# Token rows for the expert pairs: one-hot products replaced by an indirect DMA, and a weight ring of 20 slots

## The chip, the cores and the metric

One NeuronCore of a Trainium2 chip runs the whole kernel. The metric is device time in microseconds (us), the median of several runs. TensorE (PE) multiplies matrices and loads its stationary operand beside that (PEld); VectorE (DVE), ScalarE (ACT) and GpSimd (POOL) do the elementwise work; SyncE (SP) issues most of the transfers. Sixteen DMA engines move the data of all queues.

## The reference, cut to what matters

One decoder layer: four token mixers on 512 tokens of 1024 channels, merged and projected by `w_out`, then a mixture of experts. Only the last part and its routing are touched:

```python
g_prob = softmax(hf @ wg + bg);  g_p, g_idx = top_k(g_prob, 1)         # 4 groups
top_v, top_i = top_k(logits_of_that_group, 2)                          # 2 of 8 experts
gate = g_p * softmax(top_v);     expert = g_idx * 8 + top_i            # 1024 choices in all
y = (silu(xe @ w1[e]) * (xe @ w3[e])) @ w2[e]                          # per expert, D 1024, hidden 512
out[token] += gate * y
```

`hf` is the normalised residual stream, scaled by `a2` and shifted by `sh2` per channel. There are 32 experts with 6 MB of float32 weights each; all weights are read.

## The kernel before, in words

The mixers and the output projection take the first 815 us. The output projection works on two halves of the tokens (two tiles of 128 each); after each half `route` (line 1137) normalises, picks the experts of that half's tokens, and gives each choice a rank within its expert. The place of a choice is its slot: expert times 64 plus rank. Two experts make a pair, so a pair has 128 slots, and 16 pairs follow one another. Choices with a rank of 64 or more go to `overflow` (line 1403), a loop whose trip count is read from a table at run time.

How a pair gets its tokens: `route` keeps the normalised tokens as two fp16 halves (`xh`, `xl`, lines 1148 to 1162; in half 1 POOL subtracts). For two pairs at a time (a group) `rows` (line 1097) builds one-hot masks `pg` on DVE, and `gather` (line 1105) multiplies the halves with them on TensorE: 64 products of 128x256 per group, which leave the tokens transposed in PSUM. ACT and DVE then apply `a2` and `sh2` (lines 1494 and 1496) into `xe`. `tables` (line 1315) makes, for each pair, the gates `ga` (by small products `pq` and DVE steps) and the transposed mask `pT` (by four transposes `pr` and a copy on ACT).

`front` (line 1337) multiplies `xe` with the pair's w1 and w3 into `ph`, and forms g. `Back` (line 1354) transposes g (`gTp`), multiplies with w2 (`py`), scales and splits the result in two parts (`parts`), and `add` multiplies with `pT` and adds into `xm` on DVE: eight times per pair, with two products `po` each.

The weights come in 198 loads, issued by SP in order (line 1072) into a ring of 18 slots of 1 MB: ten of their own, six of the weight buffers of the stage before, and two of the buffers `ml` of the merged activations (lines 1061 to 1063). A load waits until TensorE has done with what its slot held. The order on TensorE in this stage is the order written out in the loop over pairs (line 1505 on), under a manual schedule; DVE is under one only during `route` of half 1. While `route` of half 1 runs on DVE, `meanwhile` (line 1115) gives TensorE the first half of group 0's gather and a few spare products. Once per program, `a2` and `sh2` are written to DRAM as columns and read back in another order (lines 1024 to 1031, POOL's queue).

Of the kernel before, what the change touches and what calls it, by code (L numbers as in the profile page):

```python
# [9 lines left out]
F32 = mybir.dt.float32  # L10
# [27 lines left out]
def trunk(ctx, tc, x, c, ada_w, ada_b, norm1_g, norm2_g, w_in, hgrn_lb, hgrn_norm_g, conv_w, conv_b, conv_ln_g,  # L38
# [24 lines left out]
    cst = ctx.enter_context(tc.tile_pool(name="cst", bufs=1))  # L63
    ps_mm = ctx.enter_context(tc.tile_pool(name="ps_mm", bufs=3, space=PSUM))
# [835 lines left out]
    a2c = cst.tile([128, KD], F32, name="a2c")  # L900
    sh2c = cst.tile([128, KD], F32, name="sh2c")
# [106 lines left out]
    io = keep.tile([128, 256], F16, name="io")  # L1008
    P.iota(io, pattern=[[1, 256]], base=0, channel_multiplier=0, allow_small_or_imprecise_dtypes=True)
# [52 lines left out]
    ring[RL[0]:RL[0]] = [(late, "ml")]  # L1062
    ring[RL[1]:RL[1]] = [(late, "ml")]
# [33 lines left out]
    def rows(g, p_, ts):  # L1097

        s4 = keep.tile([128, 2, NT], F32, name="s4", bufs=2)
        for t in ts:  # L1100
            V.tensor_scalar(s4[:, :, t], slot[:, 0:2, t], -256.0 * g, None, op0=OP.add)
            V.tensor_scalar(p_[:, t], io, s4[:, 0, t:t + 1], None, op0=OP.is_equal)
            V.scalar_tensor_tensor(p_[:, t], io, s4[:, 1, t:t + 1], p_[:, t], op0=OP.is_equal, op1=OP.add)

    def gather(p_, pv_, ts, ds):

        for d in ds:
            if d // 4 not in pv_:
                pv_[d // 4] = psz("xeps").rearrange("p a (b c) -> p (a b) c", c=256)
            o = pv_[d // 4][:, d % 4]  # L1110
            for t in ts:
                mm(o, xr[t][0][:, d * 128:(d + 1) * 128], p_[:, t], t == 0 and d % 2 == 0, False)
                mm(o, xr[t][1][:, d * 128:(d + 1) * 128], p_[:, t], False, t == NT - 1)

    def meanwhile(p_, pv_):


        scr = psm("scr")

        def spare(n):  # L1120
            for _ in range(n):
                mm(scr, ident, xm[:, 0, :512], True, True)

        spare(WARM[0])
        yield
        spare(WARM[1])
        for ds in ((0, 1, 2, 3), (4, 5), (6, 7)):
            gather(p_, pv_, (0, 1), ds)
            a = yield
            mm(scr[:a.shape[-1], :2], a, ident[:, :2], True, True)  # L1130
        spare(WARM[2])
        yield

    xr = []
    sq2 = nr.tile([128, NT, 4], F32, name="sq2")

    def route(half, pl, between=None):
# [5 lines left out]
        r10 = nr.tile([128, 2], F32, name="r10", bufs=2)  # L1143
        V.reduce_sum(v, sq2[:, ts], axis=AX.X)
        rsqrt(r, v, 1.0 / D)

        V.tensor_scalar(r10, r, 1024.0, None, op0=OP.mult)
        xhl = late.tile([128, 2, 2, D], F16, name="xhl", tag="mh")
        for i in range(2):
            xh, xl = xhl[:, i, 0], xhl[:, i, 1]  # L1150
            by_k = lambda a: a.rearrange("q (a p k) -> q a k p", p=128, k=4)
            in_k = lambda a: a.rearrange("q (a k p) -> q a k p", p=128, k=4)
            xi = by_k(xm[:, 2 * half + i])
            A.activation(in_k(xh), xi, AF.Copy, scale=r10[:, i:i + 1])
            if half:
                xs = nr.tile([128, D], F32, name="xs")
                A.activation(in_k(xs), xi, AF.Copy, scale=r10[:, i:i + 1])
                P.tensor_sub(xl, xs, xh)
            else:
                for a in range(2):  # L1160
                    V.scalar_tensor_tensor(in_k(xl)[:, a], xi[:, a], r10[:, i:i + 1], in_k(xh)[:, a], op0=OP.mult, op1=OP.subtract)
            xr.append((xh, xl))
        lg = nr.tile([128, 2, 36], F32, name="lg", bufs=2)
# [8 lines left out]
        el = nr.tile([128, 2, 8, 4], F32, name="el", bufs=2)  # L1172
# [22 lines left out]
        V.tensor_mul(oo, oo, pp.rearrange("p (o t e) -> p o t e", o=1, e=32).to_broadcast([128, 2, 2, 32]))  # L1195
        V.reduce_sum(rank[:, :, ts], oo, axis=AX.X)
        then(rank[:, 1, ts])
        rk, sl = rank[:, :, ts], slot[:, 0:2, ts]
        q = nr.tile([128, 2, 2], F32, name="q4", bufs=2)
        V.tensor_scalar(q, rk, 64.0, None, op0=OP.is_lt)  # L1200
        V.scalar_tensor_tensor(sl, eid[:, :, ts], 64.0, rk, op0=OP.mult, op1=OP.add)
        V.scalar_tensor_tensor(sl, sl, 1.0, q, op0=OP.add, op1=OP.mult)
        V.tensor_scalar(sl, sl, -1.0, None, op0=OP.add)
        if half:
            rows(0, first[0], (2, 3))
# [10 lines left out]
        gh, gl = (sg[:, 2:6, ts].rearrange("p (k a) t -> p a k t", a=2)[:, a] for a in range(2))
        V.tensor_scalar(gf, slot[:, 2:4, ts], 2.0 ** 15, None, op0=OP.mult)
        V.tensor_copy(gh, gf)
        V.tensor_sub(gf, gf, gh)
        V.tensor_scalar(gl, gf, 2.0 ** 11, None, op0=OP.mult)  # L1220
# [18 lines left out]
    for half in range(2):  # L1239
# [38 lines left out]
    def overflow_tables():  # L1278
# [12 lines left out]
        tmp32 = moe.tile([128, 32], F32, name="tmp32", bufs=1)  # L1291
# [20 lines left out]
    moe = ctx.enter_context(tc.tile_pool(name="moe", bufs=2))  # L1312
    ew = stream()

    def tables(p, p_):

        so = p % 2 * 128
        pr, pq = ps_mm.tile([128, 1024], F16, name="pr", tag="mm"), psm("pq")
        for t in range(NT):
            mm(pq[:, :6], p_[:, t, so:so + 128], sg[:, :, t], t == 0, t == NT - 1)  # L1320
        for t in range(NT):
            T.transpose(pr[:, t * 128:(t + 1) * 128], p_[:, t, so:so + 128], ident16)

        ga = moe.tile([128, 4], F32, name="ga")
        two = pq[:, 2:6].rearrange("p (k a) -> p a k", a=2)
        V.tensor_scalar(ga[:, 0:1], pid, 128.0 * p, None, op0=OP.add)
        V.tensor_scalar(ga[:, 1:2], pq[:, 0:1], ga[:, 0:1], 2.0 ** -15, op0=OP.is_equal, op1=OP.mult)
        V.tensor_copy(ga[:, 2:4], two[:, 0])
        V.scalar_tensor_tensor(ga[:, 2:4], two[:, 1], 2.0 ** -11, ga[:, 2:4], op0=OP.mult, op1=OP.add)
        V.tensor_mul(ga[:, 0:1], ga[:, 1:2], ga[:, 2:3])  # L1330
        V.scalar_tensor_tensor(ga[:, 3:4], ga[:, 1:2], 2.0 ** -15, ga[:, 3:4], op0=OP.subtract, op1=OP.mult)
        V.tensor_sub(ga[:, 0:1], ga[:, 0:1], ga[:, 3:4])
        pT = moe.tile([128, 512], F32R, name="pT")
        A.activation(pT, pr[:, :512], AF.Copy)
        return ga, pT

    def front(p, ga, xe):

# [225 lines left out]
```

## Time and profile before

| | |
|---|---|
| median of 3 runs | 1344.1 us (1340.98 to 1345.77) |
| the profiled execution's own time | 1340.95 us |
| its span, first to last instruction | 1339.1 us |
| mean granted clock of TensorE | 0.978 |
| busy: TensorE, DVE, ACT, POOL | 95%, 54%, 35%, 15% of the span |
| DMA | 292.99 MB, mean 219 GB/s |

A row of the timeline gives the start, the duration of a merged run of like instructions, engine, line, operation, output and input; what stands in brackets is the idle time of the engine just before, and what ended it. Matmuls are pipelined, so the duration of a run is a little longer than the distance to the next run's start. Windows give busy times in a stretch, the granted clock as a share of 2.4 GHz (0.5 is 1.2 GHz), and the mean busy share and rate of the DMA engines.

### The profile page before, as it was taken

To read this page: it belongs to the slowest core of one execution; us is meant where nothing else is said; L and a number is where in the kernel's file an instruction comes from. 1 tells how busy PE (TensorE), PEld (TensorE's weight loads), DVE (VectorE), ACT (ScalarE), POOL (GpSimd) and SP (SyncE) were. 2 spreads that over 40 slices of the span, in tenths; PEclk is the share of its full clock that TensorE was granted. 3 is DMA by queue.
4 is the path that set the end of the run, shared out by engine and by line. 5 is a ranking of instruction groups with operands and counts; after the bars stand their busy time and mean duration, and the time that the engine had idled before them with its cause. 6 is when DMAs were issued, how large, how long until landed. Compare 5 with 4: busy or idle time off the path is not lost. (4 is left out here: it accounts for less than half of the span.)

```text
span 1339.1 us, 18010 instructions
## 1 busy us (share of the span) xinstructions
PE 1270.5 (95%) x7265; PEld 894.4 (67%) x7265; DVE 718.5 (54%) x1264; ACT 471.0 (35%) x651; POOL 200.7 (15%) x157
## 2 busy tenths in 40 slices
PE   7999998999999999999989998899999999999997
PEld 5789887987789887878767896243544445353534
DVE  2624579998955555479544565253343433334324
ACT  4448464454546365454314544010111111011100
POOL 3135746001010112031111201000000000000000
PEclk9999998999999999999989999899999999999998
DMA  9432211122122232257764584999999999999961
GB/s 340 131 99 88 71 64 32 64 66 93 63 84 75 63 95 92 66 187 241 186 201 133 190 333 169 379 369 420 395 420 395 418 410 420 395 409 420 397 213 64
DMA packets 105633, 292.99 MB, mean 219 GB/s; under 512 B 8408, under 2 KB 63800, under 8 KB 81740
## 3 DMA queue, kind: packets, MB, share of 16 engines
q1 hardware_dynamic: 102312, 289.45, 57.6%
q10 hardware_dynamic: 2724, 2.26, 0.5%
q8 instruction: 58, 0.95, 0.3%
q0 software_dynamic: 512, 0.12, 0.1%
q14 instruction: 27, 0.22, 0.0%
HBM read 289.69 MB, written 2.11 MB: 218 GB/s over the span
## 5 line engine op out<-in xcount | busy, mean ns | idle before, releaser
L58 PE MATMUL ph<-ew,xe 128*64 128x512 f32 x1024 | 222.5, 592 | 0.8 <-ACT xe L1496 0.8
L58 PE MATMUL mm<-hh,wl 128*128 128x512 f32 x448 | 176.2, 393 | 4.5 <-DVE wl L253 2.9
L58 PE MATMUL mm<-hh,wh 128*128 128x512 f32 x448 | 180.0, 402 | 0.0
L58 PE MATMUL mm<-hl,wh 128*128 128x512 f32 x448 | 175.6, 392 | 0.0
L253 DVE TENSOR_TENSOR wl<-raw,wh 128x2048 fp32r<-128x2048 f32 x55 | 129.6, 2357 | 80.2 <-ACT wh L252 80.2
L58 PEld LDWEIGHTS ph<-ew,xe 128*64 128x64 f32 x1024 | 73.3, 137 | 146.8 <-issue 145.8
L1398 DVE TENSOR_TENSOR xm<-xm,po 128x512 f32<-128x512 f32 (+1 forms) x136 | 84.9, 650 | 158.2 <-PE po L58 157.1
L252 ACT ACTIVATE wh<-raw 128x2048 fp32r<-128x2048 f32 x55 | 105.1, 1911 | 76.2 <-PE mm L58 76.0
L58 PE MATMUL mm<-wh,hh 128*128 128x256 f32 x448 | 130.0, 290 | 0.0
L58 PE MATMUL mm<-wl,hh 128*128 128x256 f32 x448 | 127.1, 284 | 0.0
L58 PE MATMUL mm<-wh,hl 128*128 128x256 f32 x448 | 127.0, 283 | 0.0
L58 PE MATMUL py<-ew,gT 128*64 128x512 f32 (+1 forms) x544 | 118.8, 591 | 5.8 <-issue 5.1
L58 PEld LDWEIGHTS mm<-hh,wh 128*128 128x128 f32 x448 | 84.9, 190 | 24.0 <-issue 7.6
L58 PEld LDWEIGHTS mm<-hh,wl 128*128 128x128 f32 x448 | 84.6, 189 | 23.3 <-DVE wl L253 3.3
L58 PEld LDWEIGHTS mm<-hl,wh 128*128 128x128 f32 x448 | 84.9, 190 | 16.8 <-DVE hl L205 0.3
L58 PEld LDWEIGHTS mm<-wh,hh 128*128 128x128 f32 x448 | 86.1, 192 | 6.0 <-issue 5.8
L58 PEld LDWEIGHTS py<-ew,gT 128*64 128x64 f32 x544 | 39.1, 143 | 75.5 <-issue 72.5
L58 PEld LDWEIGHTS mm<-wl,hh 128*128 128x128 f32 x448 | 86.2, 192 | 0.2
L58 PEld LDWEIGHTS mm<-wh,hl 128*128 128x128 f32 x448 | 86.1, 192 | 0.0
L156 ACT ACTIVATE yh<-py 128x512 fp32r<-128x512 f32 (+1 forms) x34 | 19.4, 572 | 152.8 <-DVE py L1386 152.8
L1386 DVE TENSOR_TENSOR py<-py,g2b 128x512 f32<-128x512 f32 (+1 forms) x34 | 22.7, 668 | 86.0 <-PE py L58 85.5
L1349 ACT ACTIVATE g<-ph 128x512 f32<-128x512 f32 x16 | 9.6, 598 | 165.2 <-PE ph L58 165.2
(441 smaller groups left out, 2166.9 us busy)
## 6 DMA issues: line engine op xcount, KB each, us to landing
ew<-in_expert_w_dram SPq DMA_DIRECT2D x186, 1024.0 KB, 11.4
raw<-in_w_in_dram SPq DMA_DIRECT2D x26, 1024.0 KB, 5.0
raw<-in_w_gate_dram SPq DMA_DIRECT2D x16, 1024.0 KB, 5.5
adaw<-in_ada_w_dram SPq DMA_DIRECT2D x64, 256.0 KB, 3.4
aw<-in_ada_w_dram SPq DMA_DIRECT2D x32, 256.0 KB, 5.4
raw<-in_w_branch_dram SPq DMA_DIRECT2D x8, 1024.0 KB, 5.5
raw<-in_w_out_dram SPq DMA_DIRECT2D x6, 1024.0 KB, 5.9
ew<-in_expert_w_dram SPq DMA_DIRECT2D x12, 512.0 KB, 5.9
```

Source lines behind the costliest of these rows:

```text
L58: T.matmul(o, l, r, start=start, stop=stop, skip_group_check=True)
L156: A.activation(h_ap, src, AF.Copy)
L252: a = A.activation(wh, raw, AF.Copy)
L253: v = V.tensor_sub(wl, raw, wh.bitcast(F32))
L1349: A.activation(g, ph[:, 0], AF.Sigmoid)
L1386: V.tensor_mul(py, py, g2b[:, cs])
L1398: V.tensor_add(xm[:, t, cs], xm[:, t, cs], po)
```

## The change

In `route` ACT now writes the normalised tokens in float32 into one SBUF tile (`xg0`, two passes per half), and each tile of 128 tokens is written to a DRAM buffer `xhd`. Small products with one-hot tables of expert and rank (`by_slot`) give, for all 16 pairs at once, the token of every slot (`toki`, `tok`) and its gate (`ga`). An empty slot gets the number 1024, which the bounds check of the transfer leaves out. `fetch` is an indirect DMA on POOL's queue that brings the 128 rows of a pair into one of two tiles; `turn_in` transposes them (eight transposes), applies `a2` and `sh2`, and then issues the fetch for two pairs on. `places` makes `pT` on DVE from `tok`. The freed buffers `mh` join the ring, which has 20 slots. `a2` and `sh2` are transposed on TensorE and written to DRAM as rows. The working tiles of `rsqrt` have one buffer instead of two. The overflow loop gets its tokens by the same fetch. The core of the diff:

```diff
-RL = (10, 17)
+RL = (10, 11, 18, 19)
-WARM = (1, 1, 2)
+WARM = (1, 2, 2, 2, 4)
...
-        v, y, z = (cst.tile([128, 16], F32, name=nm, bufs=2)[:, :n] for nm in ("rs_v", "rs_y", "rs_z"))
+        v, y, z = (cst.tile([128, 16], F32, name=nm, bufs=1)[:, :n] for nm in ("rs_v", "rs_y", "rs_z"))
...
-    for m, src in ((0, sh2c), (1, a2c)):
-        nc.gpsimd.dma_start(colD[m].rearrange("d p -> p d"), src)
+    xhd = dram.tile([S, D], F32, name="xhd")
+    kp = ctx.enter_context(tc.tile_pool(name="kp", bufs=1, side="right"))
+    xg = [kp.tile([128, D], F32, name="xg0")]
+    T.transpose(pm[:2 * KD, :128], m2c.rearrange("p m d -> p (m d)"), ident)
+    V.tensor_copy(rowm, pm[:2 * KD, :128])
+    nc.gpsimd.dma_start(rowM, rowm)
...
-    ring[RL[0]:RL[0]] = [(late, "ml")]
-    ring[RL[1]:RL[1]] = [(late, "ml")]
+    for r, tag in zip(RL, ("ml", "mh", "ml", "mh")):
+        ring[r:r] = [(late, tag)]
...
+    def fetch(p):
+        P.indirect_dma_start(out=xg[p % 2], out_offset=None, in_=xhd[:, :],
+                             in_offset=bass.IndirectOffsetOnAxis(ap=toki[:, p:p + 1], axis=0),
+                             bounds_check=S - 1, oob_is_err=False)
...
+        for i in range(2):
+            xs = xg[0]
+            A.activation(xs, xm[:, 2 * half + i], AF.Copy, scale=r[:, i:i + 1])
+            t = 2 * half + i
+            nc.scalar.dma_start(xhd[t * 128:(t + 1) * 128], xs)
...
         if half:
-            rows(0, first[0], (2, 3))
+            tb = psm("tb")
+            by_slot(tb[:, :16], lambda h, k_, i, j: ev[h][:, k_, i, j::2])
+            V.tensor_scalar(toki, tb[:, :16], 1024.0, None, op0=OP.add)
+            fetch(0)
+            V.tensor_scalar(tok, tb[:, :16], 1024.0, None, op0=OP.add)
+            then(tok[:, :16])
...
+    xg.append(moe.tile([128, D], F32, name="xg1", bufs=1))
+    P.memset(xg[1], 0.0)
+    fetch(1)
...
-    def tables(p, p_):
...
+    def turn_in(p):
+        pt = psz("xT").rearrange("p a (b c) -> p (a b) c", c=128)
+        xe = moe.tile([128, KD, 128], F32, name="xe", bufs=1)
+        for d in range(KD):
+            a, k = divmod(d, 4)
+            T.transpose(pt[:, d], xg[p % 2][:, a * 512 + k:(a + 1) * 512:4], ident)
+        for d in range(KD):
+            if d % 2:
+                V.tensor_scalar(xe[:, d], pt[:, d], a2s[:, d:d + 1], sh2s[:, d:d + 1], op0=OP.mult, op1=OP.add)
+            else:
+                A.activation(xe[:, d], pt[:, d], AF.Identity, scale=a2s[:, d:d + 1], bias=sh2s[:, d:d + 1])
+        if p < 14:
+            fetch(p + 2)
+        return xe
...
+        def places(self):
+            self.pT = moe.tile([128, 512], F32R, name="pT", bufs=1)
+            V.tensor_scalar(self.pT, io, tok[:, self.p:self.p + 1], None, op0=OP.is_equal)
...
+    b, nxt = None, turn_in(0)
     for p in range(16):
         if b:
             for n in range(2):
                 b.product(n)
             for n in range(2):
                 b.parts(n)
+            b.places()
+        xe = nxt
+        g = front(p, xe)
...
+        late_, b = b, Back(p, g)
+        if late_:
+            late_.add(0, (0, 1, 2))
+        if p < 15:
+            nxt = turn_in(p + 1)
+        if late_:
+            late_.add(0, (3,))
+            late_.add(1, (0,))
         b.turn()
         if late_:
+            late_.add(1, (1, 2, 3))
```

## Rows read from the trace of the kernel before

**Rows 1.** Windows of the expert stage: engines' busy us, PEclk, DMA share, GB/s.
```profile
core 0: us, PE busy (x) PEld busy (x) DVE busy (x) ACT busy (x) POOL busy (x), PEclk, DMA share, GB/s
...
900.00:960.00 60.00, 58.22 (x306) 27.07 (x303) 23.06 (x57) 7.20 (x13) 0.00 (x0) 0.97 0.99 406
...
1200.00:1260.00 60.00, 58.22 (x306) 27.62 (x304) 22.54 (x47) 7.79 (x14) 0.00 (x0) 0.97 1.00 414
1260.00:1301.00 41.00, 39.22 (x186) 14.76 (x184) 14.02 (x32) 4.18 (x7) 0.00 (x0) 1.00 0.76 280
```

**Rows 2.** A window of 20 us in which the DMA engines never pause.
```profile
920.00:940.00 20.00, 20.00 (x93) 6.71 (x90) 4.31 (x13) 1.79 (x3) 0.00 (x0) 1.00 1.01 419
```

**Rows 3.** Waits of TensorE, 833 to 1319 us: total, times, longest.
```profile
PE pr L1322 <- DVE xm L1398: 7.1, 7, 1.0
```

**Rows 4.** Loads of the expert weights on SP's queue, and their time to landing.
```profile
L1072 SPq DMA_DIRECT2D ew<-in_expert_w_dram x198: 327/377/787, 755.3 to 1295.0; - x198
...
DMA to landing us min/median/max: 5.4/11.2/20.6
```

**Rows 5.** Timeline of TensorE at the start of the expert stage.
```profile
828.22 3.70 PE L58 MATMUL xeps<-pg,xhl 128*128 128x256 f16 x32 [1.56 <-DVE pg L1103]
...
833.04 13.95 PE L58 MATMUL ph<-ew,xe 128*64 128x512 f32 x64 [0.80 <-ACT xe L1496]
...
850.97 1.13 PE L1363 MATMUL gTp<-ident,g 128*128 128x128 f32 x4 [3.55 <-DVE g L1351]
```

**Rows 6.** Windows of 2 us there, columns as in rows 1.
```profile
838.00:840.00 2.00, 2.00 (x12) 0.62 (x10) 0.00 (x0) 0.00 (x0) 0.00 (x0) 1.00 0.84 324
...
852.00:854.00 2.00, 1.31 (x5) 0.53 (x6) 0.04 (x1) 0.60 (x1) 0.00 (x0) 0.50 0.99 410
```

**Rows 7.** Timeline of TensorE over one group of two pairs.
```profile
1164.38 7.09 PE L58 MATMUL py<-ew,gT 128*64 128x512 f32 x32
1171.30 13.90 PE L58 MATMUL ph<-ew,xe 128*64 128x512 f32 x64
...
1187.22 3.67 PE L58 MATMUL xeps<-pg,xhl 128*128 128x256 f16 x32
...
1191.65 0.63 PE L1363 MATMUL gTp<-ident,g 128*128 128x128 f32 x4
...
1196.67 0.38 PE L1322 MATMUL pr<-ident,pg 128*128 128x128 f16 x4
1196.98 7.09 PE L58 MATMUL py<-ew,gT 128*64 128x512 f32 x32
...
1221.69 0.38 PE L1322 MATMUL pr<-ident,pg 128*128 128x128 f16 x4 [1.01 <-DVE xm L1398]
...
1226.41 5.80 PE L58 MATMUL py<-ew,gT 128*64 128x512 f32 x26
```

**Rows 8.** Timeline of DVE, then ACT, in the routing of half 1.
```profile
816.59 0.16 DVE L147 TENSOR_TENSOR rr<-rs_y,rs_z 128x2 f32<-128x2 f32 x1
...
825.00 0.17 DVE L1203 TENSOR_SCALAR slot<-slot 128x4 f32<-128x4 f32 x1
...
816.99 2.15 ACT L1154 ACTIVATE xhl<-xm,r 128x1024 f16<-128x1024 f32 x1 [1.02 <-DVE r L1147]
```

**Rows 9.** Timeline of TensorE at the end: front of pair 15, its last products.
```profile
1294.14 13.90 PE L58 MATMUL ph<-ew,xe 128*64 128x512 f32 x64
...
1319.16 6.41 PE L58 MATMUL py<-ew,gT 128*64 128x256 f32 x32 [5.08 <-issue]
```

**Rows 10.** A contiguous pass of ACT over a token tile, at the kernel's start.
```profile
L211 ACT ACTIVATE sq<-xt x4: 1057/1057/1057, 9.5 to 15.8; 128x1024 f32<-128x1024 f32 x4
```

**Rows 11.** DMA issues of the whole span: count, KB each, us to landing.
```profile
xm<-in_x_dram SPq DMA_DIRECT2D x4, 512.0 KB, 3.8
...
mod<-colD POOLq DMA_DIRECT2D x1, 8.0 KB, 6.6
```

**Rows 12.** Timeline of DVE, then TensorE, in the routing of half 0.
```profile
786.18 4.39 DVE L1161 SCALAR_TENSOR_TENSOR xhl<-xm,r,xhl 128x512 f16<-128x512 f32 x4 [0.91 <-ACT xhl L1154]
...
798.10 0.20 PE L58 MATMUL pl<-ohb,trib 128*128 128x32 bf16 x2 [1.80 <-DVE ohb L1186]
```

More of the change, by code (lines that the diff above doesn't have):

```diff
@@ L1095, in first_max, with meanwhile @@
         return mx, idx, oh
[L1097 to L1115, printed above, removed]
+    def meanwhile():
         scr = psm("scr")
-        def spare(n):
+        for n in WARM:
             for _ in range(n):
                 mm(scr, ident, xm[:, 0, :512], True, True)
-        spare(WARM[0])
+            a = yield
+            if a is not None:
+                mm(scr[:a.shape[-1], :2], a, ident[:, :2], True, True)
         yield
[L1126 to L1134, printed above, removed]
+    def fetch(p):
+        P.indirect_dma_start(out=xg[p % 2], out_offset=None, in_=xhd[:, :],
+                             in_offset=bass.IndirectOffsetOnAxis(ap=toki[:, p:p + 1], axis=0),
+                             bounds_check=S - 1, oob_is_err=False)
     sq2 = nr.tile([128, NT, 4], F32, name="sq2")
+    oR, oE, ev, gv = [], [], [], []
     def route(half, pl, between=None):
@@ L1142, in route @@
         r = nr.tile([128, 2], F32, name="rr", bufs=2)
-        r10 = nr.tile([128, 2], F32, name="r10", bufs=2)
         V.reduce_sum(v, sq2[:, ts], axis=AX.X)
         rsqrt(r, v, 1.0 / D)
[L1147 to L1163, printed above, removed]
+        lg = nr.tile([128, 2, 36], F32, name="lg")
         for i in range(2):
             V.scalar_tensor_tensor(lg[:, i], pl[:, i * 36:(i + 1) * 36], r[:, i:i + 1], crow, op0=OP.mult, op1=OP.add)
+        for i in range(2):
[3 more added lines that the diff above has]
+            nc.scalar.dma_start(xhd[t * 128:(t + 1) * 128], xs)
         gm, gi, og = first_max(lg[:, :, :4], 4, "f0")
@@ L1211, in route, with by_slot @@
         V.scalar_tensor_tensor(gs, dv, 1.0, gs, op0=OP.add, op1=OP.mult)
-        V.reciprocal(slot[:, 2, ts], gs)
-        V.tensor_mul(slot[:, 3, ts], slot[:, 2, ts], dv)
-        V.tensor_copy(sg[:, 0:2, ts], slot[:, 0:2, ts])
+        V.reciprocal(gates[:, 0, ts], gs)
+        V.tensor_mul(gates[:, 1, ts], gates[:, 0, ts], dv)
         gf = nr.tile([128, 2, 2], F32, name="gf", bufs=2)
[L1216 to L1220, printed above, removed]
+        gh = nr.tile([128, 2, 2, 2], F16, name="gh", bufs=2)
+        V.tensor_scalar(gf, gates[:, :, ts], 2.0 ** 15, None, op0=OP.mult)
+        V.tensor_copy(gh[:, 0], gf)
+        V.tensor_sub(gf, gf, gh[:, 0])
+        V.tensor_scalar(gh[:, 1], gf, 2.0 ** 11, None, op0=OP.mult)
+        gx = nr.tile([128, 2, 2, 2, 32], F16, name="gx", bufs=2)
+        for a in range(2):
+            V.tensor_mul(gx[:, a], oe, gh[:, a, :, :, None].to_broadcast([128, 2, 2, 32]))
+        gv.append(gx)
+        if half:
+            tg = psm("tg")
+            for a in range(2):
+                by_slot(tg[:, 16 * a:16 * a + 16], lambda h, k_, i, j: gv[h][:, a, k_, i, j::2], a == 0)
+            V.tensor_scalar(ga, tg[:, 16:32], 2.0 ** -11, None, op0=OP.mult)
+            V.tensor_add(ga, ga, tg[:, :16])
+            V.tensor_scalar(ga, ga, 2.0 ** -15, None, op0=OP.mult)
+    def by_slot(o, what, first=True):
+        n = 0
+        for h in range(2):
+            for k_ in range(2):
+                for i in range(2):
+                    for j in range(2):
+                        mm(o[64 * j:64 * j + 64], oR[h][:, k_, i], what(h, k_, i, j), first and n == 0, n == 7)
+                    n += 1
     def logits(half, pl, n, cb, fill=None):
@@ L1265, in trunk @@
             pe_order.enter_context(tc.manual_schedule(engines={mybir.EngineType.PE}))
-            first = keep.tile([128, NT, 256], F16, name="pg", tag="pg"), {}
-            rows(0, first[0], (0, 1))
-            between = meanwhile(*first)
+            between = meanwhile()
         logits(half, pl, 3, cbs[3], between)
@@ L1312, in trunk, with front @@
     moe = ctx.enter_context(tc.tile_pool(name="moe", bufs=2))
+    xg.append(moe.tile([128, D], F32, name="xg1", bufs=1))
+    P.memset(xg[1], 0.0)
+    fetch(1)
     ew = stream()
-    def tables(p, p_):
[L1317 to L1337, printed above, removed]
-        so = p % 2 * 128
+    def turn_in(p):
[12 more added lines that the diff above has]
+        return xe
+    def front(p, xe):
         ph = psz("ph")
@@ L1438, in overflow @@
                 mm(pg_[:, 0:1], gt_[:, t], one32[:, 0:1], t == 0, t == NT - 1)
[L1439 to L1441 removed]
+            for t in range(NT):
+                mm(pg_[:, 2:3], pr_[:, t], tv16[:, t:t + 1], t == 0, t == NT - 1)
+            go = moe.tile([128, 2], F32, name="go")
+            V.tensor_copy(go[:, 0:1], pg_[:, 0:1])
+            V.tensor_scalar(toki[:, 0:1], pg_[:, 2:3], 1024.0, None, op0=OP.add)
+            fetch(0)
+            V.tensor_scalar(go[:, 1:2], pg_[:, 2:3], 1024.0, None, op0=OP.add)
+            pT = ewx.tile([128, 512], F32R, name="ovpT", tag="ew")
+            V.tensor_scalar(pT, io, go[:, 1:2], None, op0=OP.is_equal)
+            xo = moe.tile([128, KD, 128], F32, name="xe", bufs=1)
             ps = psz("ovx")
@@ L1444, in overflow @@
                 o = ps[:, d // 4, (d % 4) * 128:(d % 4) * 128 + 128]
-                for t in range(NT):
-                    mm(o, xr[t][0][:, d * 128:(d + 1) * 128], pr_[:, t], t == 0 and d % 4 == 0, False)
-                    mm(o, xr[t][1][:, d * 128:(d + 1) * 128], pr_[:, t], False, t == NT - 1)
-                A.activation(xo[:, d, :128], o, AF.Identity, scale=a2s[:, d:d + 1], bias=sh2s[:, d:d + 1])
+                T.transpose(o, xg[0][:, d // 4 * 512 + d % 4:d // 4 * 512 + 512:4], ident)
+                A.activation(xo[:, d], o, AF.Identity, scale=a2s[:, d:d + 1], bias=sh2s[:, d:d + 1])
             ph = psz("ovh")
@@ L1476, in overflow @@
             V.tensor_scalar(base, base, 128.0, None, op0=OP.add)
-    def group(g):
-        if g:
-            p_, pv_ = keep.tile([128, NT, 256], F16, name="pg", tag="pg"), {}
-            rows(g, p_, range(NT))
-        else:
-            p_, pv_ = first
-        yield
-        xe = moe.tile([128, KD, 256], F32, name="xe", bufs=1)
-        gr[:] = p_, xe
-        for dd in range(2):
-            for t in (range(NT),) if g else ((2,), (3,)):
-                gather(p_, pv_, t, range(4 * dd, 4 * dd + 4))
-            for d in range(4 * dd, 4 * dd + 4):
-                o = pv_[dd][:, d % 4]
-                if dd:
-                    V.tensor_scalar(xe[:, d], o, a2s[:, d:d + 1], sh2s[:, d:d + 1], op0=OP.mult, op1=OP.add)
-                else:
-                    A.activation(xe[:, d], o, AF.Identity, scale=a2s[:, d:d + 1], bias=sh2s[:, d:d + 1])
-            yield
-    gr = []
-    for _ in group(0):
-        pass
-    p_, xe = gr
-    nxt, b = tables(0, p_), None
+    b, nxt = None, turn_in(0)
     for p in range(16):
@@ L1510, in trunk @@
                 b.parts(n)
-        ga, pT = nxt
-        g = front(p, ga, xe)
+            b.places()
+        xe = nxt
+        g = front(p, xe)
         if p == 1:
             eobi, oslot = overflow_tables()
-        gg = group(p // 2 + 1) if p % 2 and p < 15 else iter(())
-        next(gg, None)
-        if b:
-            b.add(0)
-        next(gg, None)
-        if p < 15 and not p % 2:
-            nxt = tables(p + 1, p_)
-        if b:
-            b.add(1, (0, 1))
-        late_, b = b, Back(p, g, pT)
+        late_, b = b, Back(p, g)
[6 more added lines that the diff above has]
+            late_.add(1, (0,))
         b.turn()
         if late_:
-            late_.add(1, (2, 3))
-        if p % 2 and p < 15:
-            next(gg, None)
-            p_, xe = gr
-            nxt = tables(p + 1, p_)
+            late_.add(1, (1, 2, 3))
     pe_order.close()
```

84 lines of the change are left out of this document (43 added, 41 removed).

## The prediction, made before the changed kernel was run

> **What bounds the kernel now.** I read the stage of the expert products first, because the change sits in it and just ahead of it. It runs from the first up-products of pair 0 at 833.04 us to the last product of pair 15, and then a tail follows. In the windows of 60 us [rows 1] TensorE is busy 58.22 us of 60, and the DMA engines are busy 99 to 100% at 406 to 414 GB/s. So two clocks run almost level. The question is which one the change speeds up.
>
> The TensorE clock: front(0) starts at 833.04 [rows 5], front(15) at 1294.14 [rows 9], 461.1 us for 15 pairs, or 30.74 us a pair. In the waits of TensorE no transfer of weights appears; the largest is DVE's add ahead of `pr` [rows 3]. So TensorE sets the pace.
>
> The stream clock: a pair needs 12 loads of 1024 KB, 12.58 MB. In a window in which the engines never pause they move 419 GB/s [rows 2]; I use 420. That makes 29.96 us a pair, only 0.8 us below TensorE's 30.74. All 198 loads go out between 755.3 and 1295.0 us with a median of 11.2 us to landing [rows 4], so several are always queued. Only the two ends have air: the engines stand still until slots come free after front(0) has begun (324 GB/s at 838 to 840) [rows 6], and from 1260 to 1301 they are 76% busy [rows 1], since the loads there wait for slots.
>
> **TensorE, part by part.** One group of two pairs [rows 7]: the odd pair takes 1164.38 to 1196.98, 32.6 us, the even one to 1226.41, 29.4 us. Removed are the one-hot products: two batches of 32 per group, 3.67 us each, so 3.6 us a pair; `pq` and `pr`, four tiny products and four transposes (0.38 us), about 0.5 a pair; and in even pairs the 1.01 us wait at `pr` with a smaller one at `pq`, about 0.7 a pair on average. Added are eight transposes of 128x128; four take 0.63 us, so eight at most 1.3; I take 1.0. Alone this gives 30.74 - 3.6 - 0.5 - 0.7 + 1.0 = 26.9 us. But what remains between two fronts is eight products `po`, each followed by a DVE add into xm, and DVE must do 8 adds, two operations on g and four of the eight affine steps there. Three PSUM buffers let TensorE run ahead by only three adds. I therefore take 27.5 us, with 26.9 and the even pair's 29.4 as ends. pT, now made on DVE from the table, lies under the 13.90 us of front [rows 7] and costs nothing; without that cover it would be one 128x512 operation per pair. The row masks `pg` and the `ga` steps leave DVE too, so DVE does not get fuller.
>
> **The stream, part by part.** A gather replaces no transfer: it adds bytes. 512 tokens by two choices fill 1024 of 2048 slots, so 64 rows of 4 KB a pair, 0.262 MB, or 0.62 us of the stream at 420; empty slots are skipped by the bounds check. Ends: nothing (fits in gaps), and all 128 rows, 1.25 us. Fourteen of them (the first two precede the stream's restart) cost 8.7 us. The transfer of each gather is issued two pairs ahead, about 55 us before its transposes, so its wait is hidden; POOL has nothing else in this stage. The ring of 20 lets two more 1 MB loads finish while the routing runs and the stream stands still: 2.10 MB, 5.0 us.
>
> **The start.** At 816.75 DVE has the row scale rr [rows 8]. Before, ACT then made two halves in fp16 at 2.15 us each, DVE reached the slots at 825.00, and 32 products from 828.22 [rows 5] led to front(0) at 833.04. After, a chain of transfers stands there. ACT writes xs in one contiguous pass; the like pass over 128x1024 takes 1.06 us [rows 10]. Both token tiles of a half pass through the one buffer xg0, so the second pass waits for the first write to land, and the gather, on POOL, waits for the second write, though the slot table is done near 825. Behind the waiting second pass on ACT stands only small routing work. That is three landings in a row. No row shows a gather or such a write. The nearest are a 512 KB load from SP in 3.8 us and a small POOL transfer in 6.6 us [rows 11]; the far end is the weights' median under load, 11.2 us [rows 4]. I take 5 for the first write (prefetch still runs), 4 for the second, 5 for the gather: 816.75 + 1.06 + 5 + 1.06 + 4 + 5 = 832.9, plus transposes and affine, 2.2: 835.1 us. With 3.8 everywhere it is 832.5, with 11.2 everywhere 854.7.
>
> The Trainium skill (DMA: Bandwidth & Descriptors, section "Anatomy of one DMA — SWDGE (gpsimd) path") puts one such DMA at about 2.0 us plus bytes over 436 GB/s. As an estimate from that page 0.52 MB takes 3.2 us, three of them 9.6 instead of my 14, and the sum would be 4.4 us lower.
>
> In half 0, DVE loses the four operations of 4.39 us, after which TensorE waited 1.80 us for the one-hots [rows 12]; of that I count 1.5 us (ends 0 and 3.5), so front(0) starts at about 834. The wait for the first gather leaves TensorE idle for some 8 us. After a 3.55 us wait before, the granted clock was 0.50 at 852 to 854 [rows 5, 6], its 1.2 GHz level. I charge front(0) 3 us for it, 2.5 of them before the first slots come free.
>
> The sixteen small products that make the slot table, about 1 us, and the 32 for the gates lie under the wait for the second write: 0; if the writes landed at once they would be 1 us of the path. The bounce of a2 and sh2, one transpose and one copy with its two DMAs on POOL, lies under the output projection: 0; the old two DMAs lay there too. The single rsqrt buffers add only waits off this path: 0, at most 1 us either way. SP's loads are passed by nothing; POOL loses two subtractions and issues the gathers instead.
>
> **The sum.** TensorE's clock: 834 + 3 + 13.9 + 15 x 27.5 + 3.5 (pair 0 waits for g as before) = 1267 for the end of front(15). The stream's clock: before, slots came free 3.7 us after the start and the full rate stood at about 838.5, so now at 834 + 5.5 + 2.5 = 842. Loads 20 to 189 end with the last one that front(15) needs: 166 of 1.0486 MB and 4 of half that, 176.2 MB, 419.4 us. Gathers 8.7. In pair 0 the slots run out once, 4 us. One per cent for gaps, 4 us. 842 + 419.4 + 8.7 + 4 + 4 = 1278, and 2 us for the last products: 1280. The stream is later than TensorE by 13 us: TensorE, sped up by some 49 us, is late no more, and the weights are late next, in the last three or four pairs. From the end of front(15) to the end of the span it was 1339.1 - 1308.0 = 31.1 us (with 5.08 us of the overflow check [rows 9]); nothing in that changes. 1280 + 31 = 1311 us of span. The profiled execution had 1340.95 us for a span of 1339.1, and lies 3.15 below the median of the runs: 1311 + 1.85 + 3.15 = 1316 us.
>
> **Rivals.**
> - TensorE and DVE keep the bound at the even pair's 29.4 us: 834 + 3 + 13.9 + 441 + 3.5 = 1295, plus 31.1 and 5: 1331. For it: the adds that follow each other. Against: the even pair's period contains `pq`, `pr` and their waits. 0.15.
> - The three landings each take the 11.2 us of the loaded stream: 20 us more, 1336. For it: writes share engines with prefetch until about 826. Against: the engines are free after. 0.12.
> - The bounds check skips nothing that costs time, and all 128 rows move: 8.7 us more, 1325. 0.05.
> - Slower: the gather's rows go over few DMA engines. A weight load is done when its slowest engine is done. One engine moves 420/16 = 26.25 GB/s, so 64 rows on 4 engines cost 2.5 us a pair, 14 times, 35 us: 1342, no gain left. From below 4 engines it is slower; on one, 10 us a pair, 1447. No row shows which engines a transfer uses. 0.08. The Trainium skill (same page, section on the semaphore's 16) says that 128 partitions spread over 16 engines; that speaks against it, and no row here can show it.
>
> **The numbers.** The forecast, the stream as the bound, has 0.60. A measurement of this kernel can tell about 0.3% (4 us) from no change. Faster by more: forecast, first and third rival and most of the second, 0.86. Within: 0.05. Slower: the last rival and the worst of the second, 0.09. Low end 1304: start at 831, full clock, no gaps, gathers free. High end 1338: the second rival with its rest.
>
> **What would show it.** Right: front(0) at 831 to 838, at half clock for its first microseconds; pairs near 27.5 us at first and near 30.6 at the end, with waits of TensorE for `ew`; DMA 1.0 to the end; last load landing 10 us after front(15)'s last. Wrong: DMA share under 0.97 after 900 us, waits on `xg`, or front(0) after 845.

## The result, and the profile after

The changed kernel took a median of 1298.45 us (1295.56 to 1301.55, 4 runs), the kernel before 1343.87 us beside it (1340.98 to 1345.77, 4 runs): a ratio of 0.9664, with a 95% interval of 0.9634 to 0.9695. It is 45.4 us faster. 1316 us was forecast, with a range of 1304 to 1338: the direction was right, the range was not, and the kernel is faster than its low end. The profiled execution took 1301.55 us for a span of 1299.8.

First the page's row of transfers over the span, 40 slices of 33.5 us before and of 32.5 us after, then windows of the expert stage, which answer to [rows 1, 2]; the columns are those of [rows 1].

```profile
GB/s 340 131 99 88 71 64 32 64 66 93 63 84 75 63 95 92 66 187 241 186 201 133 190 333 169 379 369 420 395 420 395 418 410 420 395 409 420 397 213 64
```

```profile
GB/s 337 130 120 66 97 40 59 33 97 66 77 86 66 98 65 73 89 90 211 234 232 185 92 386 342 246 416 419 420 418 419 420 419 419 419 419 419 420 403 161
```

```profile
960.00:1020.00 60.00, 58.35 (x272) 23.53 (x273) 23.44 (x43) 8.22 (x16) 1.99 (x2) 1.00 1.01 419
1200.00:1260.00 60.00, 55.55 (x248) 23.06 (x246) 21.42 (x38) 8.22 (x16) 0.00 (x0) 1.00 1.01 418
```

The reader is to see that the weight stream now runs without a pause, at 416 to 420 GB/s from 845 to 1235 us, where the page before has slices of 395 between those of 420. TensorE, busy 58.35 us of 60 in the middle, falls to 55.55 late in the stage. What it waits for then stands in the waits of TensorE over the whole span (total, times, longest), which answer to [rows 3], and in its timeline:

```profile
PE po L58 <- DVE xm L1408: 12.4, 30, 0.6
PE ph L58 <- DMA ew<-in_expert_w_dram: 6.6, 7, 1.3
```

```profile
994.45 13.90 PE L58 MATMUL ph<-ew,xe 128*64 128x512 f32 x64
...
1022.11 3.17 PE L58 MATMUL ph<-ew,xe 128*64 128x512 f32 x14
...
1140.94 3.65 PE L58 MATMUL ph<-ew,xe 128*64 128x512 f32 x16 [0.26 <-DMA ew<-in_expert_w_dram]
1145.92 3.65 PE L58 MATMUL ph<-ew,xe 128*64 128x512 f32 x14 [1.33 <-DMA ew<-in_expert_w_dram]
...
1255.00 14.62 PE L58 MATMUL ph<-ew,xe 128*64 128x512 f32 x64
...
1280.18 5.72 PE L58 MATMUL py<-ew,gT 128*64 128x256 f32 x32 [4.74 <-SPq L1418]
```

From front(6) at 994.45 to the next at 1022.11 a pair takes 27.7 us, without a wait for weights; before, [rows 7] gave 32.6 and 29.4. The first wait for `ew` comes at 1140.94, in front(11), and from there to front(15) at 1255.00 the pairs take 29.9 to 31.2 us. The 4.74 us ahead of the last row is the overflow check, as in [rows 9].

The start, which answers to [rows 5]: TensorE, ACT with its queue, and POOL.

```profile
824.45 1.95 PE L1333 MATMUL xT<-ident,xg 128*128 128x128 f32 x8 [4.41 <-DMA xg<-xhd,toki]
827.00 15.62 PE L58 MATMUL ph<-ew,xe 128*64 128x512 f32 x64 [0.60 <-ACT xe L1338]
```

```profile
806.16 1.15 ACT L1145 ACTIVATE xg<-xm,rr 128x1024 f32<-128x1024 f32 x1 [0.82 <-DVE rr L148]
807.34 0.33 ACTq L1147 DMA_DIRECT2D xhd<-xg  x1
816.09 1.15 ACT L1145 ACTIVATE xg<-xm,rr 128x1024 f32<-128x1024 f32 x1 [8.12 <-DMA xhd<-xg]
817.27 0.33 ACTq L1147 DMA_DIRECT2D xhd<-xg  x1
```

```profile
820.76 1.09 POOL L1124 DMA_INDIRECT xg<-xhd,toki  x1 [47.78 <-DVE ga L1220]
```

The issues of transfers, with KB each and the median of us to landing, answer to [rows 4, 11]:

```profile
ew<-in_expert_w_dram SPq DMA_DIRECT2D x186, 1024.0 KB, 19.9
...
xg<-xhd,toki POOLq DMA_INDIRECT x16, 8.1
...
rowM<-rowm POOLq DMA_DIRECT2D x1, 8.0 KB, 5.3
```

Loads of weights now queue for 19.9 us, as the stream is behind. At the start there are three landings in a row, as forecast (TensorE, ACT and POOL above): 8.75 us from the first write's issue to the second pass, 3.5 from the second write to the fetch, 3.7 from the fetch to the transposes. (The releaser named in the POOL row is not the real one: fetch(0) reads xhd, whose last write was issued at 817.27, and it goes out 3.5 us after that write in four more runs.) Windows of 2 us show what the DMA engines and the clock did meanwhile, answering to [rows 6]:

```profile
808.00:810.00 2.00, 2.00 (x8) 0.76 (x6) 1.69 (x10) 0.00 (x0) 0.00 (x0) 1.00 0.98 389
820.00:822.00 2.00, 0.04 (x3) 0.00 (x0) 0.88 (x5) 0.00 (x0) 1.24 (x2) 0.54 0.00 0
828.00:830.00 2.00, 2.00 (x8) 0.63 (x6) 0.94 (x3) 1.13 (x3) 0.00 (x0) 0.50 0.48 131
832.00:834.00 2.00, 2.00 (x12) 0.69 (x10) 0.00 (x0) 0.00 (x0) 0.00 (x0) 1.00 0.35 49
```

The slow first write shared the engines with ring loads (0.98 busy at 808); the other two landings had them almost alone. TensorE, with 0.6 us of work between 818 and 824, was granted 0.50, its 1.2 GHz level, until about 830, in front(0)'s first microseconds.

All this is in the forecast. What is not in it lies ahead: DVE has the row scale `rr` of the last half at 805.97 us, where before it was 816.59 [rows 8].

```profile
805.97 0.16 DVE L148 TENSOR_TENSOR rr<-rs_y,rs_z 128x2 f32<-128x2 f32 x1
```

To separate the two parts the table divides each profiled execution there.

| kernel | median us | rr at | rr to front(0) | front(0) to the end of front(15) | rr to the span's end | TensorE's waits for ew |
|---|---|---|---|---|---|---|
| before | 1343.9 | 816.6 | 16.5 | 475.0 | 522.5 | none listed |
| after | 1298.5 | 806.0 | 21.0 | 442.6 | 493.8 | 6.6 |
| after, once more | 1295.9 | 799.5 | 20.9 | 442.5 | 493.9 | 6.1 |
| b_rows | 1334.0 | 808.3 | 16.5 | 476.1 | 523.5 | none listed |
| a_cols | 1313.3 | 818.3 | 21.2 | 442.7 | 494.3 | 6.8 |
| a_colsh | 1307.5 | 810.6 | 21.1 | 442.3 | 493.8 | 6.2 |
| a_cola2 | 1306.7 | 810.5 | 21.0 | 442.9 | 494.6 | 7.8 |
| a_colsact | 1313.8 | 816.9 | 21.0 | 442.9 | 493.7 | 6.6 |
| a_ring18 | 1300.2 | 803.7 | 20.8 | 446.2 | 498.1 | 9.8 |
| a_nofetch | 1286.0 | 800.3 | 21.0 | 432.0 | 483.3 | none listed |
| a_fetch2 | 1307.9 | 802.0 | 21.0 | 453.7 | 504.4 | 13.8 |
| a_pe1 | 1300.1 | 800.8 | 21.3 | 449.3 | 497.9 | none listed |
| a_xs2w | 1296.1 | 799.6 | 21.0 | 442.6 | 493.9 | 6.6 |
| a_gate | 1291.9 | 803.2 | 15.9 | 443.0 | 490.1 | 6.4 |

From rr on, the two executions of the changed program agree within 0.1 us, and the four versions in which only transfers ahead of rr differ lie at 493.7 to 494.6; rr itself came at 799.5 and at 806.0. So a step inside the stage is best read in the trace from rr on, and a step ahead of it from medians of runs. The change took 28.7 us from the stage (522.5 to 493.8), which leaves about 17 of the 45.4 us ahead of it, of which 1.5 were forecast.

What differs there is the bounce of sh2 and a2 through DRAM. The kernel before issues its two column writes on POOL's queue in the middle of the mixers:

```profile
637.93 0.99 POOL L1026 DMA_DIRECT2D colD<-sh2c  x1
667.46 0.90 POOL L1026 DMA_DIRECT2D colD<-a2c  x1 [28.54 <-DVE a2c L930]
```

Windows just after them, and the waits of its DVE:

```profile
640.00:642.00 2.00, 2.00 (x10) 1.65 (x10) 2.00 (x4) 0.33 (x1) 0.00 (x0) 1.00 1.88 243
642.00:644.00 2.00, 2.00 (x11) 1.65 (x10) 0.72 (x2) 0.00 (x0) 0.00 (x0) 1.00 0.41 7
...
640.00:645.00 5.00, 5.00 (x23) 4.13 (x23) 2.72 (x4) 0.56 (x2) 0.00 (x0) 1.00 1.00 110
645.00:650.00 5.00, 5.00 (x23) 4.13 (x22) 0.75 (x1) 2.46 (x3) 0.00 (x0) 1.00 0.59 44
...
670.00:675.00 5.00, 3.50 (x11) 2.79 (x12) 2.56 (x5) 0.00 (x0) 3.47 (x3) 0.78 0.16 22
```

```profile
DVE adacc L914 <- DMA adaw<-in_ada_w_dram: 29.0, 11, 11.8
```

and its issues:

```profile
colD<-sh2c POOLq DMA_DIRECT2D x1, 4.0 KB, 10.9
colD<-a2c POOLq DMA_DIRECT2D x1, 4.0 KB, 9.5
```

Each column write is 4 KB in 1024 pieces of 4 bytes. Just after the first the DMA engines move 110 GB/s, then 44; after the second, 22. The busy share beside these rates does not say what holds the loads: the 1.00 of the first window is made of 1.88, more than sixteen engines can be busy, and of 0.41 at 7 GB/s, and after the second write it is 0.16. DVE waits up to 11.8 us for an `adaw` load, and TensorE falls to 3.50 us of 5. The same windows after the change:

```profile
640.00:645.00 5.00, 5.00 (x24) 4.13 (x22) 5.00 (x6) 0.69 (x1) 1.94 (x2) 1.00 0.67 217
645.00:650.00 5.00, 5.00 (x24) 4.14 (x23) 3.57 (x5) 0.95 (x1) 0.00 (x0) 1.00 0.82 257
...
670.00:675.00 5.00, 5.00 (x23) 4.13 (x23) 2.35 (x4) 1.92 (x1) 3.80 (x3) 1.00 0.78 292
```

```profile
DVE adacc L915 <- DMA adaw<-in_ada_w_dram: 25.3, 11, 4.3
```

The write in rows goes out much later, behind the last `adaw` load (issued at 691.6):

```profile
747.86 0.54 POOL L1041 DMA_DIRECT2D rowM<-rowm  x1 [3.94 <-DVE rowm L1040]
```

### The profile page after: what moved, and what is told of

It is laid out like the page before. It is cut to its first block, busy times and chain, and to the rows that moved or that the text cites. A ratio compares the mean times of both kernels' runs of the same rounds, so it can differ in the third digit from the quotient of the medians.

```text
span 1299.8 us, 17074 instructions
## 1 busy us (share of the span) xinstructions
PE 1230.8 (95%) x6818; PEld 855.0 (66%) x6818; DVE 692.3 (53%) x1105; ACT 467.0 (36%) x665; POOL 210.7 (16%) x171
## 3 DMA queue, kind: packets, MB, share of 16 engines
q0 software_dynamic: 2784, 4.31, 1.0%
## 5 line engine op out<-in xcount | busy, mean ns | idle before, releaser
L58 PE MATMUL ph<-ew,xe 128*64 128x512 f32 x1024 | 229.8, 597 | 7.2 <-DMA ew<-in_expert_w_dram 6.6
L58 PEld LDWEIGHTS ph<-ew,xe 128*64 128x64 f32 x1024 | 77.4, 138 | 156.6 <-issue 135.3
L58 PEld LDWEIGHTS mm<-hl,wh 128*128 128x128 f32 x448 | 84.2, 188 | 16.5 <-DVE hl L206 0.3
L1124 POOL DMA_INDIRECT xg<-xhd,toki x16 | 16.0, 1000 | 394.6 <-PE xT L1333 346.5
## 6 DMA issues: line engine op xcount, KB each, us to landing
ew<-in_expert_w_dram SPq DMA_DIRECT2D x186, 1024.0 KB, 19.9
```

Source lines behind the costliest of these rows:

```text
L58: T.matmul(o, l, r, start=start, stop=stop, skip_group_check=True)
L1124: P.indirect_dma_start(out=xg[p % 2], out_offset=None, in_=xhd[:, :], in_offset=bass.IndirectOffsetOnAxis(ap=toki[:, p:p + 1], axis=0), bo ...
```

## The experiments

**The bounce in columns again (a_cols), and in rows alone (b_rows).** One undoes this part of the change, the other makes it alone in the kernel before.

```diff
-    T.transpose(pm[:2 * KD, :128], m2c.rearrange("p m d -> p (m d)"), ident)
-    V.tensor_copy(rowm, pm[:2 * KD, :128])
-    nc.gpsimd.dma_start(rowM, rowm)
+    for m, src in ((0, sh2c), (1, a2c)):
+        nc.gpsimd.dma_start(rowM[m * KD:m * KD + KD].rearrange("d p -> p d"), src)
```

> The changed kernel with a2 and sh2 written to DRAM as columns again, two transfers of 1024 pieces of 4 bytes each; all else as changed. Theory: these pieces clog the DMA engines between 640 and 685 us, loads land late, and TensorE waits; the row form gave the changed kernel its earlier start of the expert stage. Then this one is 8 to 10 us slower than the changed kernel, about 1307 us, with a wait of DVE for adaw of some 12 us near 675 us. Rival: the earlier start comes from the single rsqrt buffers or from another order of the work; then at most 2 us, about 1299 us.

> The kernel before with only the row form of a2 and sh2 (one transpose, one copy, one write of 16 rows of 512 bytes). Theory: 8 to 10 us faster than before, about 1335 us, since all of it lies ahead of the expert stage. Rival, as above: no change, 1344 us.

Measured: a_cols 1313.29 us (ratio 0.9761, 0.974 to 0.9782), 14.8 above after; b_rows 1333.96 (0.992, 0.99 to 0.994), 11.1 below the kernel before beside it (1345.02). By the ratios to the kernel before beside each, a_cols lies 13 us above after and 11 us above after once more (0.9678, below). The forecast direction holds, and the price was set too low. What the runs do not separate is the form of the write and its moment: in b_rows as in after the rows go out behind the `adaw` loads (at 742.57 and 747.86), and no run has a write in rows at 638 or 667 us. In the table both differ from their bases by 1 us at most behind rr (494.3 and 523.5 us to the end). DVE waits for all `adaw` loads (those of `g1p` with them) 40.5 us before, 23.7 in b_rows, 29.9 after and 48.1 in a_cols, whose row shows the loads late again:

```profile
DVE adacc L915 <- DMA adaw<-in_ada_w_dram: 35.0, 12, 13.6
```

**Which of the two writes costs (a_colsh, a_cola2).** One of them in columns, the other in a row of its own; the edit is that of a_cols, for one `src`.

> After, with sh2 alone bounced in columns (1024 pieces of 4 bytes, issued at about 640 us) and a2 in a row. Theory (each scatter holds back the loads that stand behind it for about as long as it takes, some 10 us, and each is paid once in the chain of adaw loads and VectorE up to the projections): about half of the 14.8 us of both, 1304 to 1307 us. Rival 1 (only the scatter of 640 us costs, as the stretch at 1.00 of the DMA engines is its own): 1311 to 1313 us. Rival 2 (only the later one, of 667 us, costs, as adaw is waited for right behind it): 1298 to 1300 us.

> After, with a2 alone bounced in columns (issued at about 667 us) and sh2 in a row. Theory (half each): 1304 to 1307 us. Rival 1 (only the scatter of 640 us costs): 1298 to 1300 us. Rival 2 (only that of 667 us): 1311 to 1313 us.

Measured 1307.48 (0.9731, 0.9716 to 0.9746) and 1306.68 (0.9722, 0.9707 to 0.9737): 9.0 and 8.2 us above after, half each, a little more than 14.8 together. Each row of windows stands behind its own write, of sh2 alone (issued at 636.55):

```profile
640.00:645.00 5.00, 5.00 (x23) 4.13 (x22) 1.34 (x3) 1.38 (x1) 0.00 (x0) 1.00 0.70 40
645.00:650.00 5.00, 5.00 (x24) 4.14 (x23) 0.36 (x1) 1.96 (x4) 0.00 (x0) 1.00 0.62 39
```

and of a2 alone (issued at 659.47):

```profile
665.00:670.00 5.00, 5.00 (x24) 4.14 (x23) 0.69 (x1) 1.77 (x1) 2.20 (x2) 1.00 0.39 28
```

**The queue or the pieces (a_colsact).** a_cols with `nc.scalar.dma_start`.

> After, with sh2 and a2 bounced in columns as in the kernel before, but issued on ACT's queue instead of POOL's. Theory (1024 pieces of 4 bytes occupy the DMA engines and hold back every other transfer, whatever queue issues them): 12 to 15 us slower than after, 1310 to 1314 us. Rival (it is POOL's queue, with its descriptors made in software, that is slow): 1298 to 1303 us.

Measured 1313.84 (0.9772, 0.9737 to 0.9807): the same as a_cols, on a queue that is not POOL's. The rival falls. That it is the pieces is argued, not isolated: 4 KB at the stream's 420 GB/s would be gone in 0.01 us, and the low rates last some 8 us behind each write of the kernel before (642 to 650, 670 to 678), but the moment of issue was not varied with the form. The pieces themselves can be counted here: ACT's queue (q10) carries 5380 packets, where in a_cols it has 3300, and two writes have 2048 pieces. The row of the page, and that of the same window:

```profile
q10 hardware_dynamic: 5380, 4.37, 1.1%
...
640.00:645.00 5.00, 5.00 (x23) 4.14 (x23) 3.06 (x3) 0.69 (x1) 0.00 (x0) 1.00 0.73 49
```

**What a gather costs the stream (a_nofetch, a_fetch2).**

```diff
         if p < 14:
-            fetch(p + 2)
```

```diff
         if p < 14:
             fetch(p + 2)
+            fetch(p + 2)
```

> The changed kernel without the gathers of pairs 2 to 15 (left out: the tokens of these pairs, which stay those of pairs 0 and 1). Theory, the gathers' bytes queue in a full stream: 14 times 0.62 us, 8.7 us less, about 1290 us; if all 128 rows move it is 17.5 us. Rival, the gathers lie in gaps or TensorE bounds the stage: 1298 us, at most 1 us less.

> After, with each of the 14 gathers of pairs 2 to 15 issued twice in a row into the same tile. Theory (once the ring's credit is used up every byte beside the weights delays the stream, and a gather of some 64 valid rows costs 0.76 us of it): 10 to 13 us slower, 1308 to 1312 us, TensorE's waits for ew growing from 6.6 us to about 17. Rival (the gathers fit into gaps of the stream, and what the run without them won was something else): 0 to 2 us slower.

Measured 1285.96 (0.9567, 0.9549 to 0.9584) and 1307.93 (0.9728, 0.9702 to 0.9754). From rr on it is 10.5 us less and 10.5 us more than after (483.3 and 504.4 against 493.8 and 493.9): 0.75 us for each of 14 gathers, in both directions, so the weight stream pays for every one. Without them no wait of TensorE for `ew` is listed, and front(15) ends 432.0 us after front(0): that is TensorE's own clock. With twice as many, the waits of TensorE grow to 13.8 us (17 was forecast) and begin at 1082 instead of 1140.94:

```profile
PE ph L58 <- DMA ew<-in_expert_w_dram: 13.8, 12, 1.4
```

**More work for TensorE (a_pe1).**

```diff
             late_.add(1, (1, 2, 3))
+            po = psm("po")
+            mm(po, ident, xm[:, 0, :512], True, True)
```

> After, with one more float32 product of 128x128 by 128x512 (two matmuls of the rows scr<-xm,ident, 0.8 to 0.9 us) at the end of each of 15 pairs' work: 12 to 13.5 us of TensorE time that nothing reads. Theory (in the second half of the expert stage the weight stream sets the pace, and TensorE with no gathers in the stream's way would end 10.6 us sooner, as the run without gathers showed): TensorE's own clock moves from front(0) + 431 to + 444, the stream's stays at + 442, so 0 to +3 us, 1298 to 1302 us, and TensorE's waits for ew fall from 6.6 us to under 2. Rival (TensorE or VectorE still sets the pace): +12 us or more, 1310 us or more.

Measured 1300.05 (0.9674, 0.9657 to 0.9692), 1.6 above after; from rr on 4.0 us more. The stage itself grew by 6.7 us (449.3) and the tail gave back 3. TensorE's own clock was 432.0, and no wait for `ew` is listed, so TensorE sets the pace here: the products, with the PSUM buffer that they take, cost it 17 us (more than the 13.5 at most that I had set), of which 10.6 lie under the stream. The rival's 12 us do not appear. The row of the late window shows TensorE filled up, 57.94 against 55.55 us, and the stream no longer quite full:

```profile
1200.00:1260.00 60.00, 57.94 (x265) 23.18 (x262) 22.46 (x40) 8.83 (x17) 0.00 (x0) 1.00 1.01 414
```

**The ring back at 18 (a_ring18).**

```diff
-RL = (10, 11, 18, 19)
+RL = (10, 17)
-    for r, tag in zip(RL, ("ml", "mh", "ml", "mh")):
+    for r, tag in zip(RL, ("ml", "ml")):
```

> The changed kernel with the ring of 18 slots again. Theory, the stream of weights bounds the stage: two loads of 1.05 MB move behind the restart of the stream, 5 us at 420 GB/s, about 1303.5 us. Rival, TensorE with DVE's adds bounds it: no change, 1298 us.

Measured 1300.24 (0.9669, 0.9652 to 0.9686): by the runs not to be told from after. By the trace from rr on it is 4.2 us later (498.1), and the waits for `ew` are 9.8 us instead of 6.6. The theory's direction holds in the trace alone.

**The start (a_xs2w, a_gate).** First the second pass through a buffer of its own, and the tables a little sooner:

```diff
-WARM = (1, 2, 2, 2, 4)
+WARM = (1, 2, 2, 1, 2)
-            xs = xg[0]
+            xs = g1b if half and i else xg[0]
```

> After, with the last token tile normalised into another buffer (g1b), so that its pass need not wait for the write of the tile before it out of xg0, and with three spare products fewer ahead of the slot tables. Theory (the landing of the last xhd write and the tables, one after the other, set front(0), and the weight stream, whose ring stands full from 820 us on, can go on only when front(0) frees a slot): the second pass starts some 8 us earlier, its write lands at about 816, the tables are there at 814 to 816, the first fetch goes out at about 816.5 instead of 820.8, front(0) and the end come 3.5 to 5 us earlier: 1293.5 to 1295 us. Rival (front(0) is held by the table and by the fetch's own time, not by the write): 0 to 1 us, 1297.5 to 1298.5 us.

Measured 1296.14 (0.9641, 0.9628 to 0.9654), between the two expectations; but from rr on nothing has moved (21.0 us to front(0), 493.9 to the end), so the gain that I forecast is not there. ACT's queue and POOL show where it went:

```profile
801.00 0.33 ACTq L1147 DMA_DIRECT2D xhd<-xg  x1
802.04 0.33 ACTq L1147 DMA_DIRECT2D xhd<-g1b  x1
...
814.47 1.09 POOL L1124 DMA_INDIRECT xg<-xhd,toki  x1 [47.91 <-DVE big L1314]
```

```profile
808.00:810.00 2.00, 0.65 (x24) 0.47 (x19) 1.30 (x10) 0.20 (x1) 0.00 (x0) 1.00 1.04 432
812.00:814.00 2.00, 0.00 (x0) 0.00 (x0) 0.28 (x1) 0.00 (x0) 0.00 (x0) 0.50 0.21 82
```

Both writes go out by 802.04, the table is there at 808.3, and yet the fetch goes out at 814.47: the engines are full of ring loads until 812, and I took the writes to land only when these are through, so that the wait for the buffer had hidden a wait for the engines. To test it, the last three ring loads were held back, by a small write of a row of gx ahead of them on SP:

```diff
+            nc.sync.dma_start(held, gx[:1].rearrange("p a k i e -> p (a k i e)"))
...
+            load_to(17)
```

> The kernel of the earlier second pass (g1b, three spare products fewer), with the last three of the 20 first ring loads held back on SP until the slot tables and fetch(0) are out (a write of one row of gx stands ahead of them on SP's queue). Theory (what the earlier pass won was lost again because its write, issued at 802 us, had to share the DMA engines with ring loads until 812 us; the DMA engines then stood idle for some 13 us with the ring full, so three loads of 2.5 us can move there for nothing): the write lands before the tables (808 us in that run), fetch(0) goes out at 808.5 instead of 814.5, front(0) and the end come 4.5 to 6 us earlier than in that run: 1290 to 1292 us. Rival 1 (a write on ACT's queue takes 8 to 12 us to land whatever else moves): 1295 to 1297 us. Rival 2 (the held loads come late and the stream loses what front(0) wins): 1295 to 1299 us with front(0) early.

Measured 1291.86 (0.9611, 0.9584 to 0.9638), as forecast. Neither rival holds: front(0) comes 15.9 us after rr instead of 21.0, and the whole from rr on takes 490.1 us, 3.8 less than after (4.5 to 6 was forecast). The writes went out at 804.61 and 805.65; the fetch, 7.2 us behind the second, now follows the table (toki at 811.87), and the engines stood idle before it, from 810 on:

```profile
812.89 1.09 POOL L1125 DMA_INDIRECT xg<-xhd,toki  x1 [42.81 <-DVE gates L1203]
```

```profile
810.00:812.00 2.00, 1.83 (x20) 0.71 (x18) 0.13 (x2) 0.00 (x0) 0.00 (x0) 1.00 0.00 0
```

```profile
814.32 0.25 SPq L1217 DMA_DIRECT2D held<-gx  x1
814.62 20.25 SPq L1087 DMA_DIRECT2D ew<-in_expert_w_dram  x11
```

This version is faster than both kernels.

**The changed kernel once more (after_again).**

> The changed kernel once more, unaltered, with more rounds, since every step of a few us is told against its time, which was known to 4 us either way. If the earlier second pass alone brought nothing (its trace says so: front(0) 20.8 us after the router's rsqrt in both), this is within 1.5 us of that run's 1296.1 us; if it brought the 2.3 us between the two medians, 1297.5 to 1299.5 us. The run with the last three ring loads held back (1291.9 us) should stay 4 us or more below it either way.

Measured 1295.93 (0.9678, 0.966 to 0.9696), beside a kernel before of 1339.8 us, 4 us below that of the first comparison. By its time a_xs2w equals it, by the ratio it is 0.4% better; from rr on they are the same. What it gained, if anything, stays open.

## Why the prediction was right and wrong

**The mechanism was right.** TensorE, sped up, no longer sets the end; the weights do, and only in the last third of the stage. The runs without, with and with twice the gathers show it from one side, the added products from the other. From rr on the forecast was 1311 less 815.25 (816.75 less the 1.5 of half 0), or 495.8 us; it measured 493.8. That the two are so close is in part luck: against the forecast the start came out 2.3 us longer, the stage 3.4 and the tail 0.9 shorter.

**The terms inside it.**
- Start: 21.0 us from rr to front(0), forecast 18.75. The landings took 8.75, 3.5 and 3.7 where I had 5, 4 and 5. By the Trainium skill's fixed price with 436 GB/s (DMA: Bandwidth & Descriptors, "Anatomy of one DMA — SWDGE (gpsimd) path") they would be, as an estimate, 9.6 together. They were 16, and the first shows what such a price leaves out: it shared the engines.
- TensorE's pair: 27.7 us, forecast 27.5; the half clock came as forecast, and front(0) took 15.6 us against 13.9, 1.7 more where I had charged 3.
- Stream: front(0) to the end of front(15) 442.6 us, forecast 446. A gather is 0.75 us, not 0.62, or 10.5 instead of 8.7; the ring 4.2, not 5.0 (by the trace). Load 20 went out 5.4 us after front(0), not 8. With 419.4 us of loads that leaves 7.3 us for the stall of pair 0, gaps and last products, where I had 10: the stall did not come, as TensorE's first wait for `ew` is at 1140.94.
- Tail: 30.2 us, forecast 31.1.
- Only the valid rows move: the page's queue of POOL carries 4.31 MB, of which 16 gathers of 64 rows are 4.19.

**The step that failed** is "The bounce of a2 and sh2, one transpose and one copy with its two DMAs on POOL, lies under the output projection: 0; the old two DMAs lay there too." The old two did not: POOL issued them at 637.93 and 667.46, as soon as their sources were there, 114 and 85 us ahead of that projection's first product (752.3), in the stretch where DVE lives on `adaw` loads. I had placed them by the program's lines, without their rows, and so put them at 0. They were worth 11.1 us in b_rows and 14.8 in a_cols (11 to 13 by the ratios). For the new write the term was right: it goes out at 747.86, beside the projection. 1316 less these is 1301 to 1305, less the 2 us that the stage came out better 1299 to 1303; the spread ahead of rr covers the rest. The 1.5 us for half 0 were not tried alone: with the columns back, rr is at 816.9 to 818.3, against 816.6 before, so no such gain is seen, but the spread ahead of rr (6.5 us) would hide it.

The Trainium skill has the rule that I passed by (DMA: Bandwidth & Descriptors, "Rules for kernel authors"): a non-contiguous last dimension makes one descriptor for each element. The traces agree: a_colsact has 2080 packets more on ACT's queue for two writes of 1024 elements. To landing, 4 KB in columns took 10.9 us in the kernel before, 8 KB as rows 5.3 us after, at another moment. The same page ("Issuing engines are not separate DMA queues") holds that transfers issued from different engines interleave on the same 16; a_colsact agrees, with 1313.84 us against 1313.29.

**The rivals.** The bound at 29.4 us a pair fell (27.7), as did three landings of 11.2 (16 us in all), all 128 rows (4.31 MB), and rows over few engines (10 us a gather on one, 2.5 on four; measured 0.75).

## What to carry to other kernels

Look up the rows of every transfer that a change removes, however small: find when it is issued and who waits for a load behind it, and do not price it by its bytes alone: here 4 KB in 1024 pieces, among loads that an engine waited for, cost 8 to 9 us. When a wait for a buffer is taken away, ask what the freed transfer will share the engines with; here it gained only once prefetch loads, with idle time left for them later, stood back. Where the same program varies ahead of a stage, divide the trace at the stage's first fixed point.

## What the hardware showed that was not expected

Two writes of 4 KB in 4-byte pieces were worth 11 to 15 us of a program of 1300: behind them the engines' busy share was 0.70 at 40 GB/s (a_colsh), against 1.01 at 420 for the weights, and one issue of an `adaw` load on SP took 7.2 us (the median is 0.33). So a busy share alone does not tell that transfers get through; the GB/s beside it do. And a write of 512 KB was followed by its fetch 3.5 us after its issue beside little else (after), and 12.4 us after it beside the ring loads (a_xs2w, 802.04 to 814.47).
